# Placing streamed matmul operands at 0xc0 and held ones at 0 modulo 0x100 in a one-core decoder block

## The chip, the cores and the metric

The kernel runs on one core of one Trainium2 chip. The metric is device time in microseconds (us). Engines are named as the profile names them: PE is TensorE's matmul, PEld its weight load (LDWEIGHTS), DVE is VectorE, ACT ScalarE, POOL GpSimd, and SP issues the DMAs. A matmul has two operands in SBUF. One is loaded into the array beforehand by a weight load and is called *held* here; the other is then passed through column by column and is called *streamed*.

## What is computed

One layer of a decoder block on 256 tokens of width 1024, all in float32. The reference, cut to its skeleton:

```python
h = rmsnorm(x, g_pre_mix); z = h @ w_in                 # 1024 x 8248
# NSA: compressed, selected and windowed attention, 16 heads in 4 groups
y_nsa = gb0 * o_cmp + gb1 * o_slc + gb2 * o_win
# mLSTM over chunks with causal conv, gates and head norm
y_ml = sigmoid(o_ml) * h_ml
# cross-attention to 256 memory tokens
y_mem = memory_xattn(q_mem, mem, g_mem, w_mem_kv)
y = gm0 * (y_nsa @ w_proj_nsa) + gm1 * (y_ml @ w_proj_ml) + gm2 * (y_mem @ w_proj_mem)
x = x + rmsnorm(y @ w_out, g_post_mix)
gu = rmsnorm(x, g_pre_ffn) @ w_ffn_in                   # 1024 x 5632
x = x + rmsnorm((silu(gate) * up) @ w_ffn_down, g_post_ffn)
```

## The kernel before

**Numbers in two parts.** Nearly every large product is made in fp32r with both operands split: `split` (two instructions, ACT then DVE) writes `hi`, a rounded copy, and `lo`, the remainder. A product is then hi·hi + hi·lo + lo·hi, three matmuls. Weights come from HBM as 161 units of 128x1024 floats (512 KB each): `fetch` brings a unit to a tile `raw` (4 buffers), `parts` (L659) splits it into `whi` and `wlo` (4 buffers each).

**Four forms of product.** They differ in which operand is held.

- `fmaj` (L674): the weights are held, the activations streamed, 256 columns at a time; 24 matmuls a unit. Used with X = (`hh`, `hl`) for the projections that must come out feature by feature: 28 units and one of gate weights (`gw`). The first product with the memory tokens (`mem_k`) has the same shapes, with `mh` and `ml` streamed.
- `tmaj` (L701): the activations are held, the weights streamed, 512 columns at a time; 12 matmuls a unit. Used for `mem_v`, the values, gates, merge gates, the three branch projections, `w_out`, the first four blocks of the FFN (`ffn_gate`, `ffn_up`) and `ffn_down`.
- `fcat` (L682): for the other 36 units of the FFN input. The activations `xc` hold hi and lo side by side, so weights `hi` are held against 512 streamed columns and `lo` against 256: seven `hi` blocks, eight `lo` blocks, then the last `hi` block.
- Attention: `nsa_half` (L1185) and `ml_head` (L1097) with streamed `kk`, `pTh`/`pTl`, `ce0`/`ce1` and `vml`, of 128 to 272 columns.

**Who sets the order.** All operations are recorded first. The class `Plan` then searches an order of all engines with its own table of durations (`cost`, L238): `schedule` places, `replay` times the result, and `choose` (L532) first tries two values of a per-matmul cost and two of a slack, then makes `ROUNDS` random trials that pull forward work on which PE waited. `issue` (L586) gives out the operations in that order. The order of program work is therefore a result of the cost table and of the number of trials, and so is the buffer of a tag that a tile gets.

**Where tiles lie.** `issue` makes a tile when its first operation is given out, and the pools place slots in that order, `one`, `big`, `wpool`, `work`. In the program before, the start addresses modulo 0x100 are:

| remainder | tiles |
|---|---|
| 0xc0 | `KK` (`memt`, `kk`, `xc`), two of the three `G` (`mh`, `ml`, `qkm1`, `vml`, `u0`, `u2`), `cs` |
| 0 | `hh`, `hl`, `yh`, `yl`, `E` (`ymemt`, `ymlt`, one `wq`), `Y` (`kmem`, `vmem`, `ynh`, `ynl`, `u3`, `u4`, two `wq`), `V` (`vs`, `u5`, one `wq`), `C`, `qs`, the third `G` (`u1`, `qkm0`), all of `raw`, `whi`, `wlo`, `pTl`, `ce0`, `ce1` |
| 0x40 | `vcs` |
| 0xe0 | `pTh` |
| 0x80, 0xa0 | `pp`, `sq` and other work tiles |

Blocks within these tiles begin at multiples of 0x200 or 0x400 bytes, so a block has its tile's remainder; the groups of `kk` are 0x840 apart, and each adds 0x40.

Of the kernel before, what the change touches and what calls it, by code (L numbers as in the profile page):

```python
# [19 lines left out]
P = 128  # L20
# [148 lines left out]
class Plan:  # L169
# [67 lines left out]
    @staticmethod  # L237
    def cost(op):  # L238

        n = op.outs[0].n if op.outs else 0  # L240
        views = op.outs + op.ins
        sources = [v for v in op.ins if not v.tile.psum and v.n > 1]
        wide = op.method in ("tensor_copy", "tensor_scalar") and not any(v.tile.psum for v in op.outs)
        op.port = op.eng == "POOL" and bool(op.ins) or op.eng == "DVE" and len(sources) > 1 - wide
        op.load = 0.0
        if op.dma:
            n = views[0].n * 4
            return views[0].shape[0] * n / (230.0 if n < 2048 else 400.0)
        if op.eng == "PE":
            dtype = op.a[1].dtype  # L250
            op.load = 56.0 if dtype == BF16 else 109.0
            if op.method == "transpose":
                return n / 1.2 + 2
            if dtype == F32:
                return max(1.72 * op.a[1].n, n / 0.6 + 10)
            return n / 2.4 + (2.5 if dtype == BF16 else 13.3) + (100 if op.a[1].shape[0] <= 32 else 0)
        n = max(v.n for v in views)
        psum = any(v.tile.psum for v in views)
        pointers = sum(v.n == 1 for v in op.ins)
        part = any(v.place() != (0, P) and v.shape[0] >= 32 for v in op.outs + [v for v in op.ins if v.n > 1])  # L260
# [12 lines left out]
        return 100 + 1.4 * n if op.method == "tensor_scalar" else max(150.0, 2.1 * n - 70)  # L273
# [80 lines left out]
    def schedule(self, matmul, slack, boost):  # L354
# [50 lines left out]
        while len(order) < len(ops):  # L405
            best = None
            for e, c in avail.items():
                if c:
                    f = max(free[e], dma - self.AHEAD) if e == "SP" else free[e]
                    t = max(f, min(x[0] for x in c))  # L410
                    if best is None or t < best[0]:
                        best = (t, e)
            assert best, "no instruction can be issued"
            now, e = best
            ready = [x for x in avail[e] if x[0] <= now]
            pick = min(ready, key=lambda x: (x[1].urge + (self.SWITCH if x[1].table not in (None, table) else 0)))
            op = pick[1]
            bad = held(op) > now or [t for t in op.tiles if t.real is None and (
                t.tag.next != t.seq or not t.tag.free or t.tag.free[0][0] > now)]
            avail[e].remove(pick)  # L420
            if bad:
                offer(op)
                continue
            op.start = now
            tags = []
            for t in op.tiles:
                if t.real is None:
                    t.place = t.tag.free.pop(0)[1]
                    t.real = True
                    t.tag.next += 1  # L430
                    tags.append(t.tag)
            if op.dma:
                free[e] = now + self.ISSUE
                dma = max(now + self.LAND, dma) + op.cost
                end = dma
            else:
                cost = op.cost
                if e == "PE":
                    now = op.start = max(now, loaded + op.load)
                    loaded = now  # L440
                    if op.load == 109.0 and op.method != "transpose":
                        cost += matmul - 13.3
                end = now + cost
                if op.table not in (None, table):
                    end += self.TABLE
                    table = op.table
                free[e] = end
            op.end = end
            if op.port:
                port[e] = end  # L450
            order.append(op)
            for t in op.tiles:
                if e != "PE":
                    t.busy[e] = op, end
                t.left -= 1
                t.end = max(t.end, end + self.NEXT[op.kind] + slack)
                if not t.left:
                    t.tag.free.append((t.end, t.place))
                    t.tag.free.sort()
                    tags.append(t.tag)  # L460
            for u in op.users:
                strict = u.deps[op]
                u.ready = max(u.ready, end + latency(op, u) if strict else end if op.eng == u.eng else now)
                u.wait -= 1
# [62 lines left out]
            free[e] = op.end  # L527
        return max(op.end for op in order)

    MATMUL, SLACK, PASSES, ROUNDS = (10.0, 13.3), (60.0, 130.0), 3, 40  # L530

    def choose(self):  # L532

# [68 lines left out]
def block_kernel(ctx, tc, order, xN, xT, memN, head, cst, vec, row, wg, w1, w2, W, out):  # L602
# [79 lines left out]
    def fcat(xc, w, ps):  # L682


        hi, lo = unit(w)
        b = lambda k: slice(k * P, (k + 1) * P)
        for k in range(KD - 1):
            PE.matmul(ps, hi[:, b(k)], xc[:, k], start=k == 0, stop=False)
# [9 lines left out]
            fmaj(ps[:, j, :], xs, range(KD), unit((w, 2 * i + j)))  # L698
        return ps

    def tmaj(xs, *key, n=4, ps_new=ps_d, into=None, last=0):  # L701


        ps = [ps_new([P, 512]) for _ in range(2)]
# [9 lines left out]
                PE.matmul(ps[tb], xs[1][:, k, t], hi[:, w], start=False, stop=(k == 2 * n - 1))  # L714

        for u in range(n - last):
            w = unit((*key, u))
            for tb in range(2):
                use(u, tb, w)
        us = range(n - last, n)  # L720
        ws = [unit((*key, u), into and into[u]) for u in us]
        for tb in range(2):
            for u, w in zip(us, ws):
                use(u, tb, w)
# [57 lines left out]

    rw = one.tile([P, 520], F32, name="rw")
    wgt = work.tile([P, 1024], F32, tag="p", bufs=2, name="wgt")
    w2t = one.tile([P, 192], F32, name="w2t")
    part(0, 776)
    part(776, 1544)
    fetch(("mem_k", 1))
# [7 lines left out]
    for u in range(4):  # L796
        if u and ("mem_k", u) not in ready:
            fetch(("mem_k", u))
        raw = ready.pop(("mem_k", u)) if u else mt[:, 264:1288]
        w = [wpool.tile([P, 1024], F32R, tag=t, bufs=4, name=t) for t in ("whi", "wlo")]  # L800
        pieces = HEAD[u]
        for h in range(2):
            if h < pieces:
# [34 lines left out]
        ACT.activation(hh[:, k, :], xt[:, k, :], AF.Copy)  # L838
        DVE.tensor_sub(hl[:, k, :], xt[:, k, :], hh[:, k, :].bitcast(F32))

    vps = tmaj(M, "mem_v", ps_new=ps_s)
    with plan.later(60):
        DVE.tensor_copy(rmb, scale_rows(mn, ps_v([P, S], "rbc"), rm, after=[vps[1].tile.last_pe]))
    with plan.later(150):
# [26 lines left out]
    MC, MT = [msk[:, 384 + 16 * i:400 + 16 * i] for i in range(2)], mtb  # L871


    hid = one.tile([P, 2, NG, 32], F32, name="hid")
    POOL.memset(hid, 0.0)
    for j in range(2):

# [19 lines left out]
        bias = work.tile([P, 1], F32, tag="b1", bufs=2, name="cbias")  # L897
# [6 lines left out]
    gw = [wpool.tile([P, 1024], F32R, tag=t, bufs=4, name="gw") for t in ("whi", "wlo")]  # L904
# [192 lines left out]
    def ml_head(h):  # L1097
# [27 lines left out]
        DVE.tensor_add(num[:, 1, h, :], pn[:, 130:258], num[:, 1, h, :])  # L1125
        DVE.tensor_copy(den[:, :, h:h + 1], pn[:, 0:260].rearrange("p (a d) -> p a d", a=2)[:, :, P:P + 1])
        for tb in range(2):
            junk = work.tile([P, P], F32, tag="junk", bufs=2, name="junk")
            ACT.activation(junk, num[:, tb, h, :], AF.Square, accum_out=ssq[:, tb, h:h + 1])

    ymlt = bigt("E", 2, [P, 2, 4, S], F32R, "ymlt")
    yml = [ymlt[:, i] for i in range(2)]
# [184 lines left out]
    def scaled(name, xs, n, gz, scale, pre, root=False):  # L1317
# [95 lines left out]
    for tb, r in scaled("ffn_down", (Hidden(0), Hidden(1)), KF // 2, ((go, [z2[:, 0, :], z2[:, 1, :]]),), halves(rfd), halves(rf), True):  # L1415
# [118 lines left out]
```

## Time and profile before

| | |
|---|---|
| times of the runs shown | 543.06, 543.06 and 543.47 us; median 543.06 |
| span of the profiled execution, first to last instruction | 540.7 us |
| what lies around it (median less span) | 2.4 us |
| PE instructions | 3116 matmuls, 3116 weight loads |
| DMA, mean over the span | 97.85 MB, 181 GB/s |

The profile gives each instruction's start and duration. Matmuls overlap one another in it: the next starts while the last is still on its way through the array. So what a matmul costs PE in a dense run is not its duration but the distance from its start to the next start, called *spacing* below. All instructions carry one source line (L598, where the order is given out), and groups are told apart by tiles: `pd<-hh,wlo` writes `pd` with `hh` streamed and `wlo` held or the other way round; the columns (256 or 512) tell which. `pd` and `pss` are two kinds of PSUM buffer for the same use.

### The profile page before, as it was taken

The page shows a single profiled execution, that of the slowest core. Times are in us where ns is not written, and L with a number is a line of the kernel's source. Part 1 is how long each engine was busy: PE and PEld are TensorE (multiplying, and loading weights), DVE is VectorE, ACT ScalarE, POOL GpSimd, SP SyncE. Part 2 cuts the span into 40 slices and gives each one's busy share as a digit, 9 for nine tenths or more (in the row PEclk, how much of TensorE's full clock was granted, in tenths as well). Part 3 has the DMA queues.
Part 4 walks back from the last instruction along what each step waited for, and adds up shares of the span by engine and source line. Part 5 has one row for each costly group of instructions (what it writes and reads, how often), then busy time and mean ns, then how long its engine had stood idle before and what let it go on. Part 6 is the DMA issues. An engine that isn't in the chain of part 4 may idle for free.

```text
span 540.7 us, 8802 instructions
## 1 busy us (share of the span) xinstructions
PE 530.9 (98%) x3116; PEld 464.9 (86%) x3116; DVE 414.2 (77%) x900; ACT 340.8 (63%) x682; POOL 30.2 (6%) x43
## 2 busy tenths in 40 slices
PE   9999999999999999999999999999999999999995
PEld 9899998998989889888888888788888888888884
DVE  6795696799999998997987796965777777754543
ACT  7695695566688885966895435744555556653431
POOL 0110000010010111101120000000000000000000
PEclk9999999999999999999999999999999999999999
DMA  8995346525433264254455474834455555555512
GB/s 317 416 412 188 129 136 195 183 79 199 146 137 128 88 234 155 98 177 155 149 174 187 167 257 159 272 118 156 166 190 189 193 196 195 189 187 191 190 63 78
DMA packets 28699, 97.85 MB, mean 181 GB/s; under 512 B 3312, under 2 KB 5232, under 8 KB 28400
## 3 DMA queue, kind: packets, MB, share of 16 engines
q1 hardware_dynamic: 28656, 97.30, 50.6%
q8 instruction: 24, 0.39, 0.3%
q14 instruction: 19, 0.16, 0.1%
HBM read 95.19 MB, written 1.05 MB: 178 GB/s over the span
## 4 chain that ended last, share of the span: by engine, by line
PE 79%; DVE 9%; ACT 5%; DMA 4%; issue 2%; POOL 1%; SPq 0%; DVEq 0%; ACTq 0%
PE pd L598 41%; PE pss L598 27%; DMA raw<-in_W 4%; DVE wlo L598 2%; PE pvn L598 2%; PE sc L598 2%; ACT whi L598 1%; PE ptn L598 1%; PE ph L598 1%; DVE cy L598 1%; ACT L598 1%; DVE sc L598 1%; DVE xt L598 1%; PE psm L598 1%; PE pgf L598 1%
## 5 line engine op out<-in xcount | busy, mean ns | idle before, releaser
L598 DVE TENSOR_TENSOR wlo<-raw,whi 128x1024 fp32r<-128x1024 f32 (+1 forms) x159 | 191.7, 1210 | 83.8 <-ACT whi L598 82.4
L598 ACT ACTIVATE whi<-raw 128x1024 fp32r<-128x1024 f32 (+1 forms) x159 | 166.2, 1051 | 128.8 <-PE pd L598 64.7
L598 PE MATMUL pd<-hh,whi 128*128 128x256 f32 x208 | 59.4, 286 | 0.9 <-DVE on L598 0.9
L598 PE MATMUL pd<-hh,wlo 128*128 128x256 f32 x208 | 59.5, 286 | 0.0
L598 PE MATMUL pd<-hl,whi 128*128 128x256 f32 x208 | 59.2, 285 | 0.0
L598 PE MATMUL pd<-whi,hh 128*128 128x512 f32 x144 | 57.7, 400 | 0.0
L598 PE MATMUL pd<-wlo,hh 128*128 128x512 f32 x144 | 57.5, 399 | 0.0
L598 PE MATMUL pd<-whi,hl 128*128 128x512 f32 x144 | 57.0, 398 | 0.0
L598 PE MATMUL pss<-xc,whi 128*128 128x512 f32 x168 | 43.6, 395 | 0.0
L598 PE MATMUL pss<-whi,u 128*128 128x512 f32 x132 | 42.0, 390 | 0.0
L598 PEld LDWEIGHTS pd<-hh,whi 128*128 128x128 f32 x208 | 39.7, 191 | 1.3 <-DVE on L598 1.1
L598 PEld LDWEIGHTS pd<-hh,wlo 128*128 128x128 f32 x208 | 39.8, 191 | 0.0
L598 PEld LDWEIGHTS pd<-hl,whi 128*128 128x128 f32 x208 | 39.7, 191 | 0.1
L598 PEld LDWEIGHTS pss<-xc,whi 128*128 128x128 f32 x168 | 30.5, 188 | 5.6
L598 PE MATMUL pd<-xc,whi 128*128 128x512 f32 x120 | 32.2, 397 | 0.0
L598 PEld LDWEIGHTS pd<-whi,hl 128*128 128x128 f32 x144 | 27.1, 188 | 4.4
L598 PEld LDWEIGHTS pd<-whi,hh 128*128 128x128 f32 x144 | 27.1, 188 | 4.4 <-ACT cx L598 0.3
L598 PEld LDWEIGHTS pd<-wlo,hh 128*128 128x128 f32 x144 | 27.1, 188 | 4.3 <-DVE wlo L598 0.3
L598 DVE CUSTOM_DVE_ANT_0 sc<-sc,msk 128x16 f32<-128x16 f32 (+2 forms) x96 | 27.2, 316 | 4.2 <-PE sc L598 3.4
L598 PEld LDWEIGHTS pss<-whi,u 128*128 128x128 f32 x132 | 24.8, 188 | 5.3
L598 ACT ACTIVATE pp<-sc,mx 128x128 f32<-128x128 f32 (+1 forms) x64 | 26.7, 427 | 1.5 <-DVE mx L598 1.3
L598 PE MATMUL pss<-wlo,u 128*128 128x512 f32 x66 | 25.8, 390 | 0.0
(333 smaller groups left out, 1122.0 us busy)
## 6 DMA issues: line engine op xcount, KB each, us to landing
raw<-in_W SPq DMA_DIRECT2D x161, 512.0 KB, 3.4
w<-in_w SPq DMA_DIRECT2D x2, 1024.0 KB, 8.1
xn<-in_xN SPq DMA_DIRECT2D x2, 512.0 KB, 9.8
xt<-in_xT SPq DMA_DIRECT2D x2, 512.0 KB, 8.2
mn<-in_memN SPq DMA_DIRECT2D x2, 512.0 KB, 8.8
kk<-kk SPq DMA_DIRECT2D x8, 128.0 KB, 3.1
x<-in_xN SPq DMA_DIRECT2D x2, 512.0 KB, 3.8
memt<-in_head SPq DMA_DIRECT2D x1, 512.0 KB, 6.4
```

Of the source, the lines that this page charges most:

```text
L598: op.ins_ = getattr(op.real, op.method)(*map(arg, op.a), **{k: arg(x) for k, x in op.kw.items()})
```

## The change

Every SBUF tag is given a fixed place ahead of the first operation (`lay_out`). The table `RESIDUE` fixes a remainder for those that feed matmuls; the others follow by size. The buffers of `whi` and `wlo` grow from 1024 to 1088 floats, and a unit is written into them at a shift of 0, 32 or 48 floats (0, 0x80, 0xc0 bytes): 0 where `fmaj` holds it, (32, 0) in `fcat`, 48 by default in `tmaj`, 0 in `mem_v`, and in `ffn_down` 48 only against the `Y` tiles. To make room, `w2t` and `hid` share the slots of `ce0` and `ce1`, `cbias` has one buffer, and the tile `junk` goes (the unused squares are written over the float32 copy of a mask in `msk`, of which a bf16 copy is in use). The planner's durations for fp32r matmuls change from n/2.4 + 13.3 to 17n/38.4 + 1.5 ns, the tried offsets from (10.0, 13.3) to (-3.0, 0.0) on that base, and its random trials from 40 to 100.

```diff
-            return n / 2.4 + (2.5 if dtype == BF16 else 13.3) + (100 if op.a[1].shape[0] <= 32 else 0)
+            return (n / 2.4 + 2.5 if dtype == BF16 else n * 17 / 38.4 + 1.5) + (100 if op.a[1].shape[0] <= 32 else 0)
...
-                        cost += matmul - 13.3
+                        cost += matmul
...
-    MATMUL, SLACK, PASSES, ROUNDS = (10.0, 13.3), (60.0, 130.0), 3, 40
+    MATMUL, SLACK, PASSES, ROUNDS = (-3.0, 0.0), (60.0, 130.0), 3, 100
...
+    FIRST_BYTE = 0x4080
+    RESIDUE = {"vcs": 0, "V": 0, "C": 0, "G": 0, "qs": 0, "KK": 0xC0, "E": 0xC0, "Y": 0xC0, "hh": 0xC0, "hl": 0xC0,
+               "whi": 0, "wlo": 0, "raw": 0, "pT0": 0xC0, "pT1": 0xC0, "ce0": 0xC0, "ce1": 0xC0}
+
+    def lay_out(self, order):
...
+        for name in ("one", "big", "wpool", "work"):
+            pool, slots = pools[name]
+            for (label, n), size in sorted(slots.items(), key=lambda x: (rank.get(x[0][0], 99), x[1])):
+                pad = (self.RESIDUE[label] - place) % 0x100 if label in rank else 0
+                if pad:
+                    pool.tiles.tile([P, pad // 4], F32, tag=f"pad{place}", bufs=1, name="pad")
+                pool.tiles.tile([P, (size + 31) // 32 * 8], F32, tag=f"{label}_{n}", bufs=1, name="slot")
...
+    def room(shift=(0, 0)):
+        return [wpool.tile([P, 1088], F32R, tag=t, bufs=4, name=t)[:, n:n + 1024] for t, n in zip(("whi", "wlo"), shift)]
...
-        hi, lo = unit(w)
+        hi, lo = unit(w, shift=(32, 0))
...
-    def tmaj(xs, *key, n=4, ps_new=ps_d, into=None, last=0):
+    def tmaj(xs, *key, n=4, ps_new=ps_d, into=None, last=0, shift=lambda u: 48):
...
-    w2t = one.tile([P, 192], F32, name="w2t")
+    w2t = work.tile([P, 192], F32, tag="ce0", bufs=1, name="w2t")
...
-    vps = tmaj(M, "mem_v", ps_new=ps_s)
+    vps = tmaj(M, "mem_v", ps_new=ps_s, shift=lambda u: 0)
...
-    hid = one.tile([P, 2, NG, 32], F32, name="hid")
+    hid = work.tile([P, 2, NG, 32], F32, tag="ce1", bufs=1, name="hid")
...
-            junk = work.tile([P, P], F32, tag="junk", bufs=2, name="junk")
-            ACT.activation(junk, num[:, tb, h, :], AF.Square, accum_out=ssq[:, tb, h:h + 1])
+            ACT.activation(msk[:, K_MT - K_M0:], num[:, tb, h, :], AF.Square, accum_out=ssq[:, tb, h:h + 1])
...
+                        shift=lambda u: 48 * (tags[u // 2][0] == "Y")):
```

More of the change, by code (lines that the diff above doesn't have):

```diff
@@ L584, in choose @@
         return self.schedule(matmul, slack, boost)
+    FIRST_BYTE = 0x4080
+    RESIDUE = {"vcs": 0, "V": 0, "C": 0, "G": 0, "qs": 0, "KK": 0xC0, "E": 0xC0, "Y": 0xC0, "hh": 0xC0, "hl": 0xC0,
+               "whi": 0, "wlo": 0, "raw": 0, "pT0": 0xC0, "pT1": 0xC0, "ce0": 0xC0, "ce1": 0xC0}
+    def lay_out(self, order):
+        pools, at = {}, {}
+        for op in order:
+            for t in op.tiles:
+                if not t.psum:
+                    slots = pools.setdefault(t.pool.name, (t.pool, {}))[1]
+                    key = t.label, t.place
+                    n = t.n * (2 if t.dtype == BF16 else 4)
+                    slots[key] = max(slots.get(key, 0), n)
+        place = self.FIRST_BYTE
+        rank = {label: i for i, label in enumerate(self.RESIDUE)}
+        for name in ("one", "big", "wpool", "work"):
[5 more added lines that the diff above has]
+                pool.tiles.tile([P, (size + 31) // 32 * 8], F32, tag=f"{label}_{n}", bufs=1, name="slot")
+                at[label, n] = place + pad
+                place += pad + (size + 31) // 32 * 32
+        self.at, self.end = at, place
     def issue(self):
@@ L592, in issue @@
         with self.tc.manual_schedule():
+            self.lay_out(order)
             for op in order:
@@ L657, in fetch, with parts, unit @@
         return raw
-    def parts(raw, into=None):
-        hi, lo = into or [wpool.tile([P, 1024], F32R, tag=t, bufs=4, name=t) for t in ("whi", "wlo")]
+    def room(shift=(0, 0)):
+        return [wpool.tile([P, 1088], F32R, tag=t, bufs=4, name=t)[:, n:n + 1024] for t, n in zip(("whi", "wlo"), shift)]
+    def parts(raw, into=None, shift=(0, 0)):
+        hi, lo = into or room(shift)
         split(hi, lo, raw)
         return hi, lo
-    def unit(key, into=None):
+    def unit(key, into=None, shift=(0, 0)):
         if key not in ready:
             fetch(key)
-        return parts(ready.pop(key), into)
+        return parts(ready.pop(key), into, shift)
     def mm3(out, ah, al, bh, bl, start, stop, **kw):
@@ L716, in tmaj @@
         for u in range(n - last):
-            w = unit((*key, u))
+            w = unit((*key, u), shift=(shift(u),) * 2)
             for tb in range(2):
@@ L720, in tmaj @@
         us = range(n - last, n)
-        ws = [unit((*key, u), into and into[u]) for u in us]
+        ws = [unit((*key, u), into and into[u], (shift(u),) * 2) for u in us]
         for tb in range(2):
@@ L799, in block_kernel @@
         raw = ready.pop(("mem_k", u)) if u else mt[:, 264:1288]
-        w = [wpool.tile([P, 1024], F32R, tag=t, bufs=4, name=t) for t in ("whi", "wlo")]
+        w = room()
         pieces = HEAD[u]
@@ L896, in block_kernel @@
             PE.matmul(ph, w1t[j][:, l, :], st[:, 2 * l % 16, n:n + 80], start=(l == 0), stop=(l == 15))
-        bias = work.tile([P, 1], F32, tag="b1", bufs=2, name="cbias")
+        bias = work.tile([P, 1], F32, tag="b1", bufs=1, name="cbias")
         DVE.tensor_copy(bias, ph[:, 64:65])
@@ L903, in block_kernel @@
     pgf = ps_s([P, S], "pgf")
-    gw = [wpool.tile([P, 1024], F32R, tag=t, bufs=4, name="gw") for t in ("whi", "wlo")]
+    gw = room()
     split(gw[0], gw[1], wgt)
@@ L1315, in block_kernel, with scaled @@
     DVE.tensor_mul(gp[:, 1, :], g1, gp[:, 0, :])
[L1317 removed]
+    def scaled(name, xs, n, gz, scale, pre, root=False, **kw):
         ss = work.tile([P, 2, 2], F32, tag="ss", bufs=2, name="ss")
@@ L1323, in scaled @@
             c = slice(512 * h, 512 * h + 512)
-            for tb, ps in enumerate(tmaj(xs, name, h, n=n, ps_new=ps_ds, last=4 * h)):
+            for tb, ps in enumerate(tmaj(xs, name, h, n=n, ps_new=ps_ds, last=4 * h, **kw)):
                 sq = work.tile([P, 512], F32, tag="sq", bufs=3, name="sq")
@@ L1414, in block_kernel @@
     halves = lambda t: [t[:, tb:tb + 1] for tb in range(2)]
-    for tb, r in scaled("ffn_down", (Hidden(0), Hidden(1)), KF // 2, ((go, [z2[:, 0, :], z2[:, 1, :]]),), halves(rfd), halves(rf), True):
+    for tb, r in scaled("ffn_down", (Hidden(0), Hidden(1)), KF // 2, ((go, [z2[:, 0, :], z2[:, 1, :]]),), halves(rfd), halves(rf), True,
+                        shift=lambda u: 48 * (tags[u // 2][0] == "Y")):
         for c in (slice(0, 512), slice(512, 768), slice(768, 1024)):
```

## The prediction

> **What bounds the kernel now.** I read the page's busy table and its 40 slices first, then the chain that ended last.
>
> ```profile
> span 540.7 us, 8802 instructions
> ...
> PE 530.9 (98%) x3116; PEld 464.9 (86%) x3116; DVE 414.2 (77%) x900; ACT 340.8 (63%) x682; POOL 30.2 (6%) x43
> ...
> PE   9999999999999999999999999999999999999995
> ...
> PEclk9999999999999999999999999999999999999999
> ...
> PE 79%; DVE 9%; ACT 5%; DMA 4%; issue 2%; POOL 1%; SPq 0%; DVEq 0%; ACTq 0%
> ```
>
> PE is busy in every slice but the last, at full granted clock, and carries 79% of the chain. It idles for 540.7 - 530.9 = 9.8 us, of which 6.6 us is the tail behind the last matmul (533.73 + 0.39, below) and about 1 us the start. So time is won only where the spacing of matmuls shrinks. I therefore went to the timeline of PE alone and looked for dense runs of one form, first and last start with the count between them.
>
> ```profile
> 98.74 0.28 PE L598 MATMUL pd<-hh,wlo 128*128 128x256 f32 x1
> ...
> 102.94 0.28 PE L598 MATMUL pd<-hl,whi 128*128 128x256 f32 x1
> ```
>
> Between these lie 35 matmuls of `fmaj`: (102.94 - 98.74)/35 = 120.0 ns each. Streamed `hh`/`hl` and held `whi`/`wlo` all have remainder 0.
>
> ```profile
> 400.62 1.07 PE L598 MATMUL pd<-xc,wlo 128*128 128x256 f32 x8
> 401.53 2.02 PE L598 MATMUL pd<-xc,whi 128*128 128x512 f32 x8
> 403.39 1.07 PE L598 MATMUL pd<-xc,wlo 128*128 128x256 f32 x8
> 404.30 0.39 PE L598 MATMUL pd<-xc,whi 128*128 128x512 f32 x1
> 404.53 1.80 PE L598 MATMUL pss<-xc,whi 128*128 128x512 f32 x7
> ```
>
> Here `fcat` streams the same 256 columns, from remainder 0xc0 with `wlo` held at 0: eight take (401.53 - 400.62) = 0.91 us, 113.5 ns each. Equal shape and data type, same engine state, 6.5 ns less; the cleanest starts give 113.3, which I use (difference 6.7 ns). Each kind is the same in all its dense runs, whichever buffer it has, so the remainder is the suspect. A second pair of rows, means of single durations by group, says the same: spacing in a dense run is the duration less about 163 ns.
>
> ```profile
> L598 PE MATMUL pd<-hh,wlo 128*128 128x256 f32 x208 | 59.5, 286 | 0.0
> ...
> L598 PE MATMUL pss<-xc,whi 128*128 128x512 f32 x168 | 43.6, 395 | 0.0
> ...
> L598 PE MATMUL pd<-xc,whi 128*128 128x512 f32 x120 | 32.2, 397 | 0.0
> ...
> L598 PE MATMUL pss<-xc,wlo 128*128 128x256 f32 x168 | 22.6, 277 | 0.0
> ...
> L598 PE MATMUL pd<-whi,ynh 128*128 128x512 f32 x24 | 9.3, 389 | 0.0
> ...
> L598 PE MATMUL pss<-wlo,mh 128*128 128x512 f32 x16 | 6.3, 392 | 0.0
> ```
>
> For 512 columns the good pair is another one. `whi` streamed at 0 with `ynh` held at 0 is best (389), `xc` streamed at 0xc0 with `whi` held at 0 worst (395 and 397), `wlo` streamed at 0 with `mh` held at 0xc0 between (392). The two runs that size them:
>
> ```profile
> 318.50 0.39 PE L598 MATMUL pss<-whi,ynh 128*128 128x512 f32 x1
> ...
> 324.40 0.39 PE L598 MATMUL pss<-whi,ynl 128*128 128x512 f32 x1
> ```
>
> ```profile
> 364.22 0.39 PE L598 MATMUL pd<-whi,xc 128*128 128x512 f32 x1
> ...
> 369.94 0.39 PE L598 MATMUL pss<-whi,xc 128*128 128x512 f32 x1
> ```
>
> 26 matmuls in 5.90 us are 226.9 ns (0 streamed, 0 held); 25 in 5.72 us are 228.8 ns (0 streamed, 0xc0 held). For a whole `fcat` unit, 8 wide and 8 narrow matmuls, the rows above give 403.39 - 400.62 = 2.77 us, where 8 x 226.7 + 8 x 113.3 would be 2.72.
>
> My reading: the streamed reads and the next matmul's weight load meet in the memory, and the difference of the two start addresses modulo 0x100 sets how often. That only the difference counts is assumed, not shown: no row has both at 0xc0.
>
> **The change part by part.**
>
> *1. `fmaj`, 29 units x 24 = 696 matmuls.* `hh`/`hl` go to 0xc0, weights stay at 0: the pair of the 113.3 ns row. In full that is 696 x 6.7 = 4.6 us. Thirteen of the units stand beside the attention:
>
> ```profile
> 28.00:104.00 76.00, 75.84 (x589) 73.01 (x588) 56.07 (x107) 53.62 (x97) 2.40 (x6) 1.00 0.59 207
> 104.00:282.00 178.00, 176.81 (x1109) 155.94 (x1108) 161.45 (x510) 135.48 (x352) 22.48 (x20) 1.00 0.42 147
> ```
>
> (Stretch, length, then PE, PEld, DVE, ACT, POOL busy, clock, DMA share, GB/s.) From 28 to 104 us DVE is busy 56.07 of 76 us, so the 16 units there keep the full gain, 384 x 6.7 = 2.6 us. From 104 to 282 us DVE is busy 91% and runs of one form are short; I count 5 ns, 312 x 5 = 1.5 us. If DVE's cover were gone altogether, these 1.5 us would become PE waits for `wlo`. **Taken: -4.1; bounds -4.6 and -2.6.**
>
> *2. `fcat`, 36 units.* `xc` stays at 0xc0, `whi` moves to 0x80, `wlo` stays. The streamed address is then 0x40 ahead of the held one. The nearest row with that difference is 228.8 ns (0 less 0xc0 is 0x40). Seven wide matmuls of a unit take now (403.39 - 401.53) less the one that ends the unit before, 0.226: 1.63 us, 233 ns each. Six of them are followed by a `whi` load and gain 4 ns; the seventh is followed by `wlo` as before, and the two around the last `hi` block get a new neighbour, which I let cost 3 ns each. That is about 20 ns a unit, 36 x 0.020 = 0.7. Clean spacing would give 36 x 0.05 = 1.9; 8 ns on all eight (the 397 row, against 0.05 us a unit now) would cost 0.5. **Taken: -0.8; bounds -1.9 and +0.5.**
>
> *3. Wide matmuls now with 0 streamed, 0xc0 held:* `mem_v` 48, `ffn_gate` 72 of 96, `ffn_up` 48, and `u0`, `u2` of `ffn_down` 96, together 264. They go to equal remainders, 228.8 to 226.9 ns. **Taken: -0.5; bounds -0.6 and 0.** The 24 `ffn_gate` matmuls on `V` stay as they are.
>
> *4. Narrow attention matmuls.* `pTh`, `pTl` and `ce` to 0xc0 against `vs` and `vcs` at 0, and `kmem` against `qm`:
>
> ```profile
> L598 PE MATMUL pvn<-pTh,vs 128*128 128x256 f32 x48 | 13.0, 283 | 0.0
> ...
> L598 PE MATMUL psm<-kmem,qm 128*128 128x256 f32 x24 | 3.5, 283 | 0.0
> ```
>
> 283 against 277 is 6 ns; 152 matmuls, not in long runs: at most 0.9, **taken -0.4**, at least 0. `kk`, 96 matmuls, keeps its remainders and its `qs` at 0.
>
> *5. `mem_k` turns the other way.* `mh`, `ml` go from 0xc0 to 0, so 96 matmuls get the 120 ns pair: +0.6 in full. They lie in the first 12 us, where the start waits for data as well (the chain's first long piece, then the timeline):
>
> ```profile
> 2.12 5.65 DMA raw<-in_W
> ```
>
> ```profile
> 9.06 0.62 PE L598 MATMUL pd<-ml,whi 128*128 128x256 f32 x4
> 9.52 0.62 PE L598 MATMUL pd<-mh,wlo 128*128 128x256 f32 x4
> ```
>
> Four take 0.46 us at 9 us, so PE is dense there by then; the chain has the DMA ahead of it. **Taken +0.3; bounds 0 and +0.6.**
>
> *6. All other wide matmuls* (weights streamed at shift 48 against `hh`, `hl`, `yh`, `yl`, `E`, `Y`, or `xc`): some 890 that have 0/0 now or join that class get 0xc0/0xc0. Same difference, **taken 0**. This is the largest unknown: see the third rival.
>
> *7. Splits.* ACT and DVE write `whi`/`wlo` at 0, 0x80 or 0xc0. Rows of equal shape at other remainders bear on that:
>
> ```profile
> L598 DVE TENSOR_TENSOR pTl<-ptn,pTh 128x512 fp32r<-128x512 f32 x24 | 16.0, 686 | 0.1
> ...
> L598 DVE TENSOR_TENSOR mrg<-mrg 128x512 f32<-128x512 f32 x8 | 5.5, 690 | 0.1
> ```
>
> 686 ns with an input at 0xe0 and the output at 0, 690 with all at 0x80: no effect on DVE. The shared slots of `w2t`, `hid` add waits between work 40 us apart. The squares into `msk` are ACT's own sequence; if they made DVE's mask readers wait, eight squares of some 0.3 us could cost DVE up to 2 us in its fullest stage. Taken 0.
>
> *8. The order.* New durations and 100 trials give another order. What it can win is what PE loses to waits now: 9.8 us idle less 6.6 of tail less 1 of start, 2.2 us, since the tail is fixed work:
>
> ```profile
> 533.73 0.39 PE L598 MATMUL pd<-whi,u 128*128 128x512 f32 x1
> ```
>
> It can lose as much. **Taken 0; bounds -2 and +3.**
>
> Sum: -4.1 - 0.8 - 0.5 - 0.4 + 0.3 = **-5.5 us**. The profiled span of 540.7 becomes 535.2, and with the 2.4 us around it the time is 537.6, against the median of 543.06.
>
> **A rule that speaks against it.** The Trainium skill, "TensorE: Matmul & The Clock Gate", section "Step-by-step: what each phase is for", says that PE has two independent SBUF read ports and that loading the next tile's weights "doesn't steal SBUF read bandwidth from the running matmul". By it the addresses would not matter, and terms 1 to 5 would be nothing. The 120.0 and 113.5 ns above disagree with that, unless something else tells these two forms apart.
>
> **The rivals.**
>
> - *Nothing happens* (chance 5%). The two narrow forms differ also in their rows: `fmaj` changes its streamed block every matmul between `hh` and `hl`, `fcat` walks through one tile. If that makes the 6.7 ns, all terms are 0 and the time is 543.1. Against it: `psm<-kmem,qm`, another kernel stage at 0/0, has 283 too. The rule named above gives this time.
> - *More than forecast* (17%). `fcat` becomes clean (-1.9), terms 1, 3, 4 come in full (-6.1), `mem_k` is hidden, and the longer search wins 0.5: 543.06 - 8.5 = 534.5. For it: the differences are the same in every dense run.
> - *Slower* (7%). One mechanism: what counts is not the difference but the streamed address, and 512 columns streamed from 0xc0 are the bad case, as in `fcat`. Then the 890 wide matmuls of part 6 go from 226.7 to the longer of the two `fcat` rows, 397 against 389, 8 ns more: +7.1 us, 543.06 - 5.5 + 7.1 = 544.7. It decides from 5.5 us / 890 = 6.2 ns each, that is from 232.9 ns on. For it: the only wide matmuls that stream from 0xc0 today have the longest durations, 395 and 397. Against it: narrow ones from 0xc0 have the shortest.
> - *The order eats half* (15%). The search works on other durations, DVE is full at 104 to 282 us, and PE's waits there more than double: +3, 540.6.
>
> **How the numbers follow.** Forecast, 536 to 540: 56%; more than forecast 17%; order eats half 15%; slower 7%; nothing 5%. A measurement of this kernel can tell about 0.2% (1.1 us) from no change. Faster than 541.97 are the forecast, the better case and nearly all of the fourth: 0.86. Nothing, and edges of its neighbours: 0.07. Slower: 0.07. The range from 534.2 to 541.5 leaves out the slower case, no change and the far edge of the better one.
>
> **What would show it.** Step 1: `pd<-hh,wlo` at 277 to 280 ns and dense runs at 113.3. Step 2: the wide `pss<-xc,whi` below 395, three units in less than 8.32 us. Step 3: `wlo,mh` from 392 to 389. Step 5: `mh,whi` runs longer by 6 ns. Step 6: `whi,ynh` still at 389; 395 or more there would be the slower rival and would make the forecast wrong. Step 8: PE's idle time near 9.8 us; DVE waits in the middle stage would show the fourth rival.

## The result and the profile after

The changed kernel takes 537.0 us (median of 4 runs, 536.13 to 537.46) against 543.06 us: a ratio of 0.9886, with an interval from 0.9869 to 0.9902. The forecast was 537.6. The profiled execution took 536.95 us, its span 535.2 us. In a second set of runs, made with the experiments, the same kernel took 536.38 us, a ratio of 0.9892 [0.9878, 0.9906]. The helper that gives out the work is at L627 now.

The page of the changed kernel: busy time, the DMA engines' share in 40 slices, and the chain:

```profile
span 535.2 us, 8817 instructions
...
PE 525.0 (98%) x3116; PEld 462.3 (86%) x3116; DVE 411.9 (77%) x900; ACT 342.2 (64%) x682; POOL 30.8 (6%) x43
...
DMA  8995356525524454344465575734555555555512
...
PE 87%; DVE 5%; DMA 4%; ACT 1%; issue 1%; POOL 0%; SPq 0%; DVEq 0%; ACTq 0%
```

The span falls by 5.5 us, PE's busy time by 5.9. PE now carries 87% of the chain, where it had 79%. Its idle time has not fallen: 535.2 - 525.0 = 10.2 us, 9.8 before. Everything was won inside PE's busy time. The groups of PE of the changed kernel by form (busy us, mean ns of one, idle before):

```profile
L627 PE MATMUL pd<-hh,wlo 128*128 128x256 f32 x208 | 58.5, 281 | 0.0
...
L627 PE MATMUL pss<-xc,whi 128*128 128x512 f32 x168 | 43.1, 392 | 0.0
L627 PE MATMUL pd<-xc,whi 128*128 128x512 f32 x120 | 31.9, 394 | 0.0
L627 PE MATMUL pss<-xc,wlo 128*128 128x256 f32 x168 | 22.6, 277 | 0.0
...
L627 PE MATMUL pvn<-pTh,vs 128*128 128x256 f32 x48 | 13.1, 281 | 0.0
...
L627 PE MATMUL pd<-whi,ynh 128*128 128x512 f32 x24 | 9.3, 389 | 0.0
...
L627 PE MATMUL pss<-wlo,mh 128*128 128x512 f32 x16 | 6.2, 390 | 0.0
...
L627 PE MATMUL psm<-kmem,qm 128*128 128x256 f32 x24 | 3.4, 276 | 0.0
```

`xc,whi` loses 3 ns, `wlo,mh` 2 ns, `psm` 7 ns, and `whi,ynh`, now 0xc0 against 0xc0, stays at 389. `hh,wlo` is the surprise: 281, not the 277 of `xc,wlo`, though both now stream from 0xc0 against 0. Two dense runs of `fmaj` in the timeline of PE, first and last matmul of each, show why. The first:

```profile
99.96 0.28 PE L627 MATMUL pd<-hh,whi 128*128 128x256 f32 x1
...
104.79 0.28 PE L627 MATMUL pd<-hh,wlo 128*128 128x256 f32 x1
```

These are 41 steps in 4.83 us, **117.8 ns** each. The second:

```profile
53.99 0.28 PE L627 MATMUL pd<-hl,whi 128*128 128x256 f32 x1
...
59.78 0.28 PE L627 MATMUL pd<-hl,whi 128*128 128x256 f32 x1
```

These are 51 steps in 5.79 us, 113.5 ns (113.3 after the first few). The same instructions at the same remainders run at one of two speeds, and each of the 20 dense runs of nine steps or more in the trace keeps its speed to its end. The speed isn't set by the program alone: the run of 58 steps that ends at 40.7 us goes at 117.8 ns here, and at 113.3 in a second trace of the same kernel, taken with the experiments. For `fcat`, the starts of its blocks in the same view:

```profile
401.25 1.07 PE L627 MATMUL pss<-xc,wlo 128*128 128x256 f32 x8
402.16 2.00 PE L627 MATMUL pss<-xc,whi 128*128 128x512 f32 x8
404.00 1.07 PE L627 MATMUL pss<-xc,wlo 128*128 128x256 f32 x8
...
406.74 1.07 PE L627 MATMUL pss<-xc,wlo 128*128 128x256 f32 x8
```

Two units take 406.74 - 401.25 = 5.49 us, 2.745 each, where one took 2.77.

**Where the time went.** I took the distance from each fp32r matmul of 256, 272 or 512 columns to the next start, less the best distance seen for its width (113.3, 120.4, 226.7 ns), in both traces. What is over by less than 14 ns I sum as *spacing*, what is over by more as *waits* (a wait for data, a change of form, or, in the first microseconds, matmuls of `mem_k` that still start 213 ns apart):

| us | before | after | difference |
|---|---|---|---|
| spacing, `fmaj` | 4.17 | 1.70 | -2.47 |
| spacing, `fcat`, 512 and 256 columns | 1.90 | 1.06 | -0.84 |
| spacing, wide on `xc`, `u0`, `u2`, `mh`, `ml` | 0.57 | 0.26 | -0.31 |
| spacing, narrow attention (`pvn`, `psm`) | 0.71 | 0.43 | -0.28 |
| spacing, `mem_k` | 0.10 | 0.59 | +0.49 |
| spacing, all | 9.60 | 6.19 | -3.41 |
| waits, all | 13.94 | 11.85 | -2.09 |

Together that is 5.5 us, the fall of the span. The places explain 3.4 us of it. The other 2.1 us are waits, which points to the order; the experiments below test that. They lie around `pvn` (1.64 to 0.63), `yh` (0.74 to 0.19) and `ymlt` (0.66 to 0.19). The second trace of the same kernel has 11.28 us of waits and 5.95 us of spacing. The page counts most of the waits as busy time, since an earlier matmul is still on its way while the next start is late: of the 13.94 us before, only 2.2 us are idle time.

The stretch of the attention, in the view by windows (PE, PEld, DVE, ACT, POOL busy), shows what became of the fear for it:

```profile
104.00:282.00 178.00, 177.77 (x1122) 158.25 (x1121) 161.05 (x512) 138.42 (x355) 23.06 (x20) 1.00 0.45 152
```

DVE is as full as before, and PE's idle time there went from 1.2 to 0.2 us. The idle time that came instead is at the start, in the list of what PE waited for (us in total, times, longest):

```profile
PE rbc L627 <- POOL rm L627: 1.3, 1, 1.3
PE warm L627 <- POOL mhalf L627: 1.0, 1, 1.0
PE pd L627 <- ACT whi L627: 0.8, 1, 0.8
```

In before's list `rbc` stands with 0.2 us and the third isn't listed. Both lie in the first 34 us, in the first three slices, where the DMA engines are busy for 8, 9 and 9 tenths.

### The profile page after: what moved, and what is told of

Its sections match the earlier page's. It is cut to its first block, busy times and chain, and to the rows that moved or that the text cites. A ratio compares the mean times of both kernels' runs of the same rounds, so it can differ in the third digit from the quotient of the medians.

```text
span 535.2 us, 8817 instructions
## 1 busy us (share of the span) xinstructions
PE 525.0 (98%) x3116; PEld 462.3 (86%) x3116; DVE 411.9 (77%) x900; ACT 342.2 (64%) x682; POOL 30.8 (6%) x43
## 4 chain that ended last, share of the span: by engine, by line
PE 87%; DVE 5%; DMA 4%; ACT 1%; issue 1%; POOL 0%; SPq 0%; DVEq 0%; ACTq 0%
PE pd L627 47%; PE pss L627 28%; DMA raw<-in_W 4%; PE pvn L627 3%; PE sc L627 2%; PE ptn L627 2%; PE ph L627 1%; DVE wlo L627 1%; ACT whi L627 1%; DVE xt L627 1%; PE pn L627 1%; PE pvm L627 1%; PE pgf L627 1%; PE psm L627 1%; PE pq L627 1%
## 5 line engine op out<-in xcount | busy, mean ns | idle before, releaser
L627 DVE TENSOR_TENSOR wlo<-raw,whi 128x1024 fp32r<-128x1024 f32 (+1 forms) x159 | 191.8, 1213 | 80.4 <-ACT whi L627 79.9
L627 ACT ACTIVATE whi<-raw 128x1024 fp32r<-128x1024 f32 (+1 forms) x159 | 166.2, 1052 | 116.4 <-PE pd L627 57.2
L627 PE MATMUL pd<-hh,wlo 128*128 128x256 f32 x208 | 58.5, 281 | 0.0
L627 PE MATMUL pd<-hh,whi 128*128 128x256 f32 x208 | 58.4, 281 | 0.0
L627 PE MATMUL pd<-hl,whi 128*128 128x256 f32 x208 | 58.2, 280 | 0.0
L627 PE MATMUL pd<-whi,hh 128*128 128x512 f32 x144 | 57.5, 399 | 0.0
L627 PE MATMUL pd<-wlo,hh 128*128 128x512 f32 x144 | 57.5, 399 | 0.0
L627 PE MATMUL pd<-whi,hl 128*128 128x512 f32 x144 | 56.8, 398 | 0.0
L627 PE MATMUL pss<-xc,whi 128*128 128x512 f32 x168 | 43.1, 392 | 0.0
L627 PE MATMUL pss<-whi,u 128*128 128x512 f32 x132 | 42.0, 390 | 0.0
L627 PEld LDWEIGHTS pd<-hl,whi 128*128 128x128 f32 x208 | 39.3, 189 | 0.2
L627 PEld LDWEIGHTS pd<-hh,whi 128*128 128x128 f32 x208 | 39.2, 188 | 0.2
L627 PEld LDWEIGHTS pd<-hh,wlo 128*128 128x128 f32 x208 | 39.1, 188 | 0.1
L627 PEld LDWEIGHTS pss<-xc,whi 128*128 128x128 f32 x168 | 30.5, 188 | 5.2
L627 PE MATMUL pd<-xc,whi 128*128 128x512 f32 x120 | 31.9, 394 | 0.0
L627 DVE CUSTOM_DVE_ANT_0 sc<-sc,msk 128x16 f32<-128x16 f32 (+2 forms) x96 | 27.2, 313 | 5.2 <-PE sc L627 4.5
L627 PEld LDWEIGHTS pd<-whi,hh 128*128 128x128 f32 x144 | 27.1, 188 | 4.5 <-ACT cx L627 0.2
L627 PEld LDWEIGHTS pd<-whi,hl 128*128 128x128 f32 x144 | 27.1, 188 | 4.5
L627 PEld LDWEIGHTS pd<-wlo,hh 128*128 128x128 f32 x144 | 27.1, 188 | 4.0
L627 PEld LDWEIGHTS pss<-whi,u 128*128 128x128 f32 x132 | 24.8, 188 | 5.2
L627 ACT ACTIVATE pp<-sc,mx 128x128 f32<-128x128 f32 (+1 forms) x64 | 26.9, 434 | 1.8 <-DVE mx L627 1.7
L627 PE MATMUL pss<-wlo,u 128*128 128x512 f32 x66 | 25.7, 389 | 0.0
```

The source lines that it names most:

```text
L627: op.ins_ = getattr(op.real, op.method)(*map(arg, op.a), **{k: arg(x) for k, x in op.kw.items()})
```

## The experiments

Theory A: the difference of the two start addresses, modulo 0x100, sets the spacing, and the order gives about 2 us more. Theory B: the streamed address alone counts. Theory C: the order did it all. Diffs are against the changed kernel. Differences between kernels are taken from their ratios to the kernel before, times 542.5 us, against the changed kernel's 0.9892; each has an uncertainty of about 1 us. Of the variants of the kernel, all but the last two have the changed kernel's order on PE.

**Spacing by itself.** Only series of 24 matmuls from one tile; the streamed block starts at `m`, the held ones at `h`. Each series comes after 9 wide matmuls, directly or with a small one (the entry) between.

```diff
+            tests.append((n, 0, 0x20 * s, e))
...
+    for n, m, h in ((256, 0xC0, 0), (256, 0xC0, 0xC0), (256, 0x80, 0x80), (512, 0xC0, 0), (512, 0xC0, 0xC0),
+                    (512, 0xC0, 0x80), (512, 0x40, 0), (256, 0x40, 0x80)):
+        for e in range(4):
+            tests.append((n, m, h, e))
```

> This kernel leaves out the whole block and writes its input back: it only runs series of 24 fp32r matmuls, of 256 or 512 streamed columns in the order of fmaj (streams alternate hi, lo, hi; the third weight block is another), for eight held remainders 0, 0x20 ... 0xe0 against a streamed remainder 0 and for some pairs with both moved, each after four different entries. Theory (difference of the two start addresses modulo 0x100 counts, two steady states of one pair are possible): difference 0: 120 ns at 256 columns and 226.7 at 512; difference 0xc0: 113.3 or 117.8 at 256 depending on the entry, 233 at 512; difference 0x40: 229 at 512; pairs with the same difference and other addresses have the same spacing. Rival (the streamed address alone counts): pairs with 0xc0/0xc0 behave as 0xc0/0 and not as 0/0. Rival (independent read ports): all 113.3 and 226.7.

Some of the series in its timeline of PE. First 0 against 0x40 (a difference of 0xc0) without and with an entry of 272 columns, then 0xc0 against 0xc0; then the same for 512 columns: 0xc0 against 0, and 0xc0 against 0xc0:

```profile
122.33 2.99 PE L53 MATMUL ta<-t 128*128 128x256 f32 x24
...
127.23 0.28 PE L58 MATMUL entry<-t 128*128 128x272 f32 x1
127.35 2.91 PE L53 MATMUL tb<-t 128*128 128x256 f32 x24
...
451.52 3.03 PE L53 MATMUL te<-t 128*128 128x256 f32 x24
...
492.43 5.76 PE L53 MATMUL te<-t 128*128 128x512 f32 x24
...
523.75 5.61 PE L53 MATMUL ta<-t 128*128 128x512 f32 x24
```

The mean of the last 12 distances of a series in ns, by streamed less held start modulo 0x100, with the spread over the entries:

```
difference     0      0x20   0x40   0x60   0x80         0xa0         0xc0            0xe0
256 columns  120.0  116.7  117.8  120.0  118.2-120.0  117.3-118.5  113.3 or 117.8  118.3-118.8
512 columns  226.7  233.3  228.9  233.3  232.6-233.3  233.8-234.6  233.3           233.3
```

Pairs with equal differences but other addresses agree to 0.1 ns (streamed/held): 0/0, 0x80/0x80 and 0xc0/0xc0 at 256 columns (120.0), 0/0 and 0xc0/0xc0 at 512 (226.7), 0/0xc0, 0xc0/0x80 and 0x40/0 at 512 (228.9). That decides for A's first half and against B: 512 columns streamed from 0xc0 are best against 0xc0. For 256 columns at 0xc0 there are two steady spacings. In the three pairs with that difference the entry of 272 columns led to 113.3 each time and the direct start to 117.8 each time; entries of 160 columns or of four small matmuls gave either.

The Trainium skill says in "SBUF — State Buffer", section "Who interferes with whom", that PE has two read ports, one for the matmul's moving operand and one for the weight load, and that they are independent. This grid disagrees, if that is taken to mean that the two can't disturb each other: with nothing else at work, matmuls that differ in their start addresses alone differ by up to 6.7 ns at 256 columns and 7.9 ns at 512. What in the memory or in PE makes the difference, no run shows.

**The order alone.** The changed planner, every operand at its remainder of before, no shifts.

```diff
-    RESIDUE = {"vcs": 0, "V": 0, "C": 0, "G": 0, "qs": 0, "KK": 0xC0, "E": 0xC0, "Y": 0xC0, "hh": 0xC0, "hl": 0xC0,
-               "whi": 0, "wlo": 0, "raw": 0, "pT0": 0xC0, "pT1": 0xC0, "ce0": 0xC0, "ce1": 0xC0}
+    RESIDUE = {"vcs": 0x40, "V": 0, "C": 0, ("G", 0): 0xC0, ("G", 1): 0xC0, ("G", 2): 0, "G": 0, "qs": 0, "KK": 0xC0, "E": 0, "Y": 0, "hh": 0, "hl": 0,
+               "whi": 0, "wlo": 0, "raw": 0, "pT0": 0xE0, "pT1": 0, "ce0": 0, "ce1": 0}
...
-        hi, lo = unit(w, shift=(32, 0))
+        hi, lo = unit(w)
...
-    def tmaj(xs, *key, n=4, ps_new=ps_d, into=None, last=0, shift=lambda u: 48):
+    def tmaj(xs, *key, n=4, ps_new=ps_d, into=None, last=0, shift=lambda u: 0):
...
```

> The order of the changed kernel, instruction by instruction on PE, with the remainders of before (G 0xc0, 0xc0, 0; E, Y, hh, hl, ce at 0; pTh at 0xe0; vcs at 0x40) and no shifts. If the places gave 3.4 us and the order 2.1 us, as the two traces added up, this is at 540.5 us, 3.5 us over the changed kernel. If the places gave all of the forecast's 5.5 us, it is at 543. If the order gave all, it is at 537.

540.32 us, ratio 0.9961 [0.9947, 0.9975]: the order gives 0.0039 x 542.5 = 2.1 us (with it the shared slots and the squares into `msk`, which this kernel keeps), the places the other 3.7. Its groups are back where they were (`wlo,mh` but for one late matmul of 498 ns, which lifts the mean):

```profile
L627 PE MATMUL pd<-hh,wlo 128*128 128x256 f32 x208 | 59.4, 285 | 0.0
...
L627 PE MATMUL pss<-xc,whi 128*128 128x512 f32 x168 | 43.6, 395 | 0.0
...
L627 PE MATMUL pss<-wlo,mh 128*128 128x512 f32 x16 | 6.4, 399 | 0.0
```

Spacing sums to 9.90 us (before 9.60), waits to 11.41 (before 13.94). Theory C falls, and so does the theory that the places did it all.

**`fmaj` back.** `hh` and `hl` at 0, and the weights that `tmaj` streams against them at shift 0.

```diff
-"hh": 0xC0, "hl": 0xC0,
+"hh": 0, "hl": 0,
...
-        for tb, ps in enumerate(tmaj(X, "o_ml", last=2)):
+        for tb, ps in enumerate(tmaj(X, "o_ml", last=2, shift=lambda u: 0)):
...
```

> The changed kernel with hh and hl (and so yh, yl) back at 0, and their tmaj weights streamed at 0, so that only fmaj changes its pair, from 0xc0/0 to 0/0. If fmaj gave what the trace adds up, 2.5 us, the time is 539.5; with the forecast's 4.1 us it would be 541.1. fmaj's dense runs go to 120.0 ns everywhere.

538.82 us, ratio 0.9937 [0.9922, 0.9952]: `fmaj` is worth (0.9937 - 0.9892) x 542.5 = 2.4 us. Its spacing is 4.27 us here, 1.45 and 1.70 in the two traces of the changed kernel.

**`fcat` back.** Both parts at shift 0.

```diff
-        hi, lo = unit(w, shift=(32, 0))
+        hi, lo = unit(w)
```

> The changed kernel with the hi weights of fcat back at 0. The two traces differ by 0.85 us in fcat, so 537.9 is expected; the forecast's 0.8 gives the same, clean spacing would have given 1.9. Three units go back from about 8.24 to 8.32 us.

537.53 us, ratio 0.9910 [0.9895, 0.9925]: 1.0 us for `fcat`. In the trace its spacing is 1.90 us against 1.06.

**`mem_k` back.** `mh` and `ml` at 0xc0, the wide matmuls against `G` shifted with them.

```diff
-"G": 0,
+"G": 0xC0,
...
-    vps = tmaj(M, "mem_v", ps_new=ps_s, shift=lambda u: 0)
+    vps = tmaj(M, "mem_v", ps_new=ps_s)
...
-                        shift=lambda u: 48 * (tags[u // 2][0] == "Y")):
+                        shift=lambda u: 48 * (tags[u // 2][0] != "V")):
```

> The changed kernel with the three G tiles at 0xc0, mem_v and the G part of ffn_down streamed at shift 48 against them. The trace gives mem_k 0.5 us more conflict than before, so if PE is the bound there, the time falls by 0.5 us against the changed kernel; if the start waits for data, it stays the same. The other pairs stay at difference 0.

A miss: 537.72 us, ratio 0.9914 [0.9901, 0.9928], 1.2 us slower than the changed kernel if anything. The timeline of PE shows `mem_k` faster where it is dense, and waiting for `whi` before that:

```profile
8.06 0.63 PE L627 MATMUL pd<-mh,wlo 128*128 128x256 f32 x4
9.14 0.74 PE L627 MATMUL pd<-mh,whi 128*128 128x256 f32 x4 [0.44 <-ACT whi L627]
...
11.08 0.62 PE L627 MATMUL pd<-ml,whi 128*128 128x256 f32 x4
11.54 0.62 PE L627 MATMUL pd<-mh,wlo 128*128 128x256 f32 x4
```

Four matmuls take 11.54 - 11.08 = 0.46 us, 0.48 in the changed kernel. Its spacing falls from 0.61 to 0.09 us against the second trace of the changed kernel, but its waits rise from 0.44 to 1.52: 0.61 is the late start behind the wait for `whi`, and some 0.5 are starts 213 ns apart ahead of 6.4 us. `fmaj` fell into the slower steady state more often (1.90 us against 1.45). The start waits for data here, so no gain shows. The changed kernel's first trace has the same 1.51 us of waits with the slow `mem_k`. Why this kernel came out slower and not equal isn't settled.

**`fcat` with equal remainders.** `whi` at 0xc0, the best difference for 512 columns taken alone.

```diff
-        hi, lo = unit(w, shift=(32, 0))
+        hi, lo = unit(w, shift=(48, 0))
```

> The changed kernel with the hi weights of fcat at 0xc0, so that wide matmuls have difference 0 there. Six dense wide matmuls of a unit go from 228.9 to 226.7 ns, -13 ns; the one narrow stream during which hi is loaded goes from 0x40 to 0, 117.8 to 120, +2. Sum -11 ns a unit, -0.4 us on 36. If the change of form inside a unit breaks the steady state, the difference is 0 within 0.2 us.

Another miss: 537.67 us, ratio 0.9915 [0.9900, 0.9930], 1.2 us slower where a gain was expected. Its units in the timeline:

```profile
401.66 1.11 PE L627 MATMUL pss<-xc,wlo 128*128 128x256 f32 x8
402.60 2.00 PE L627 MATMUL pss<-xc,whi 128*128 128x512 f32 x8
404.44 1.11 PE L627 MATMUL pss<-xc,wlo 128*128 128x256 f32 x8
...
407.22 1.11 PE L627 MATMUL pss<-xc,wlo 128*128 128x256 f32 x8
```

The eight narrow ones take 0.94 us, not 0.91: they have gone to the 117.8 state. The wide ones take 1.84 us in both. A unit is 2.78 us, not 2.745; 36 times 0.035 is 1.3 us (1.1 by the sum over the trace), enough for the whole loss.

**Mixed units by themselves.** A grid over the two differences that a unit mixes, `hi` and `lo`, in steps of 0x20: units of `fmaj` after three entries, and three units of `fcat`.

```diff
+    for a in range(8):
+        for b in range(8):
+            for e in (0, 1, 3):
+                tests.append(("fmaj", 0x20 * a, 0x20 * b, e))
+            tests.append(("fcat", 0x20 * a, 0x20 * b, 0))
```

> This kernel leaves out the whole block and writes its input back: it runs units of fmaj (24 matmuls) and of fcat (3 units of 16) over a grid of two differences in steps of 0x20, that of the two hi blocks and that of the lo block, fmaj after three entries (six wide matmuls; these and one of 272 columns; these and two plain fp32 ones). Theory (difference between a stream and the weights loaded during it counts, and 0xc0 at 256 columns has two steady states, 113.3 and 117.8 ns): 0xc0/0xc0 ends in either of them by the entry; other pairs of differences have one state, and some of these may be below 117.8 for every entry. For fcat 0x40/0xc0 (the changed kernel) 2.75 us a unit, 0xc0/0xc0 (before) 2.77, 0/0xc0 about 2.74. Rival (the entry does not matter, the order of tiles in the real kernel does): all entries alike.

Mean of the last 12 distances of `fmaj` by entry, and the time of a `fcat` unit, from the starts in its trace (ns):

```
differences hi, lo    fmaj, three entries      fcat unit
0xc0, 0xc0            117.8  113.3  117.8      2773
0x40, 0xc0            113.3  113.3  113.3      2747
0xc0, 0x40            113.3  113.2  113.3      2803
0,    0xc0            117.8  117.8  117.8      2780
0,    0               -      120.0  120.1      2794
others                115.5 to 124.4           2757 to 2827
```

(The first series of 0, 0 is left out: it lies at the start of the kernel, and its first 11 distances are 213 ns.) So the changed kernel has the best of the 64 pairs for `fcat`, and equal remainders are worse than before's pair. For `fmaj` two pairs reach 113.3 from every entry, and the kernel's isn't one of them.

**Locking `fmaj`.** `lo` at shift 32, which makes the differences 0xc0 and 0x40.

```diff
-            fmaj(ps[:, j, :], xs, range(KD), unit((w, 2 * i + j)))
+            fmaj(ps[:, j, :], xs, range(KD), unit((w, 2 * i + j), shift=(0, 32)))
...
-    gw = room()
+    gw = room((0, 32))
```

> The changed kernel with the lo weights of fmaj (and of the gate unit) at 0x80, so that its two differences are 0xc0 for hi and 0x40 for lo. The grid shows 113.3 ns there after every entry, where 0xc0/0xc0 stays at 117.8 after some. If the remaining 1.5 us of conflict in fmaj is this second steady state, dense runs are at 113.3 everywhere and the time falls by 1.2 to 1.5 us against the changed kernel, to about 535.0. If the waits for ACT and DVE take the gain, it stays at 536.4.

536.06 us, ratio 0.9884 [0.9868, 0.9900], span 533.7 us. In the trace the mechanism works: a stretch that ran at 117.8 in the changed kernel's trace (34.02 to 36.38 us there, 20 steps in 2.36) now reads

```profile
33.30 0.28 PE L627 MATMUL pss<-hh,whi 128*128 128x256 f32 x1
...
37.95 0.28 PE L627 MATMUL pd<-hh,wlo 128*128 128x256 f32 x1
```

41 steps in 4.65 us, 113.4 ns. The spacing of `fmaj` falls from 1.45 to 0.54 us. In the time it can't be told from the changed kernel (-0.4 us). One cause shows in the trace: `mem_k`'s waits were 1.52 us in this execution, of which 0.6 are starts 213 ns apart, and 0.44 in the second trace of the changed kernel. From the first start of `fmaj` to the end this execution took 504.4 us, the two of the changed kernel 506.2 and 506.6. That is one execution against two; the median is the lowest of all kernels here, no more.

**The wide matmuls at a bad difference.** The default shift of `tmaj` at 32, so that 768 wide matmuls (720 on `hh`, `hl` and the `y` tiles, 48 of `ffn_up`) stream from 0x80 against 0xc0.

```diff
-    def tmaj(xs, *key, n=4, ps_new=ps_d, into=None, last=0, shift=lambda u: 48):
+    def tmaj(xs, *key, n=4, ps_new=ps_d, into=None, last=0, shift=lambda u: 32):
```

> The changed kernel with the weights of tmaj streamed at 0x80 instead of 0xc0 against tiles at 0xc0: some 720 wide matmuls get difference 0xc0. This is the price of the rival that forecast slower. If the difference counts, each dense one goes from 226.7 to 233.3 ns: +4.5 to +4.8 us, 541. If the streamed address alone counts, 0x80 is another case and nothing says which.

538.25 us, ratio 0.9919 [0.9905, 0.9933]: only 1.5 us slower. Where runs are long the price is in full, as the timeline shows:

```profile
318.41 0.39 PE L627 MATMUL pss<-whi,ynh 128*128 128x512 f32 x1
...
320.98 0.39 PE L627 MATMUL pss<-whi,ynl 128*128 128x512 f32 x1
```

That is 11 steps in 2.57 us, 233.6 ns each, where 226.7 stood. But the spacing of these forms rises by 3.0 us in all, not by 768 x 6.6 ns = 5.1: the 432 matmuls on `hh` and `hl`, in short runs beside the attention, were some 3 ns over the best already (1.30 us) and lose only 1.1 us more. And `fmaj` fell into its better state more often (0.81 us against 1.45), and the waits were 10.40 us against 11.28; the edit doesn't aim at either, and whether the other addresses ahead of `fmaj` led to them isn't settled.

**Trials, and the planner of before.** First 40 trials in place of 100; then the durations, offsets and trials of before, with the new places.

```diff
-    MATMUL, SLACK, PASSES, ROUNDS = (-3.0, 0.0), (60.0, 130.0), 3, 100
+    MATMUL, SLACK, PASSES, ROUNDS = (-3.0, 0.0), (60.0, 130.0), 3, 40
```

> The changed kernel with 40 random trials instead of 100, so another order of all engines from the same durations. If the longer search gave the 2.3 us that the order brought, this is at 538 or above; if the durations gave them, at 536.5 to 537.

537.58 us, ratio 0.9913 [0.9899, 0.9928], 1.1 us slower. But its waits at `mem_k` were 2.40 us in the trace, 2.0 more than in the second trace of the changed kernel, and they are no waits for data:

```profile
8.03 1.05 PE L627 MATMUL pd<-mh,whi 128*128 128x256 f32 x4
8.88 1.05 PE L627 MATMUL pd<-ml,whi 128*128 128x256 f32 x4
...
10.44 0.64 PE L627 MATMUL pd<-mh,whi 128*128 128x256 f32 x4
10.91 0.64 PE L627 MATMUL pd<-ml,whi 128*128 128x256 f32 x4
```

Four matmuls take 8.88 - 8.03 = 0.85 us, and 10.91 - 10.44 = 0.47 two blocks later. The slow ones, 213 ns each, make 2.1 of the 2.40 us. They end at 10.2 us in this trace, at 6.7 in the trace of before, at 5.1 in the first trace of the changed kernel, and the second has none, so the moment can differ between executions of one kernel. From the first start of `fmaj` to the end this execution took 505.5 us, less than the changed kernel's 506.2 and 506.6. Only one of the six executions was traced, so the slower median may have other causes too; what the trials alone give isn't settled.

```diff
-            return (n / 2.4 + 2.5 if dtype == BF16 else n * 17 / 38.4 + 1.5) + (100 if op.a[1].shape[0] <= 32 else 0)
+            return n / 2.4 + (2.5 if dtype == BF16 else 13.3) + (100 if op.a[1].shape[0] <= 32 else 0)
...
-                        cost += matmul
+                        cost += matmul - 13.3
...
-    MATMUL, SLACK, PASSES, ROUNDS = (-3.0, 0.0), (60.0, 130.0), 3, 100
+    MATMUL, SLACK, PASSES, ROUNDS = (10.0, 13.3), (60.0, 130.0), 3, 40
```

> The changed places with the durations, offsets and 40 trials of before. If places and order add, this is 2.3 us over the changed kernel, 538.7; if the order only pays together with the places, it is nearer to 536.4 or above 539.

539.15 us, ratio 0.9942 [0.9928, 0.9956]. The places alone give 0.0058 x 542.5 = 3.1 us, and the planner 2.7 us on top of them. Spacing is 5.82 us, waits 13.87 (before 13.94). With the order alone, above, all four corners are there: 2.1 or 2.7 us for the order, 3.1 or 3.7 for the places. They add within the uncertainty of about 1 us.

## Why the prediction was right

The time was forecast to 0.6 us (537.6 for 537.0), the span to the tenth. The rule that the places were chosen by was right, but the closeness of the sum is luck: two terms were off in opposite directions, `fmaj` by 1.6 us too much and the order by 2.1 to 2.7 us too little.

- **Only the difference counts** (assumed for parts 2, 3 and 6): shown, by the grid of pairs and by `whi,ynh` at 389. The change in the spacing of all forms of part 6 is about 0, as taken. That the streamed reads and the weight load "meet in the memory" stays a reading; no run looks inside.
- **Term 1, `fmaj`: mis-sized.** Taken -4.1, bounds -4.6 and -2.6; measured -2.4 by undoing it and -2.5 in the trace, just outside. The step that failed is the reading of one spacing from the `fcat` row. Its narrow matmuls come each time after wide ones, and sit in the faster of two states; `fmaj` starts after all sorts of work and fell into the slower one in many of its runs. So the loss lies in both stretches: 28 to 104 us was taken with 2.6 us and gave 1.5, 104 to 282 us with 1.5 and gave 1.0 (spacing 2.29 to 0.77 and 1.88 to 0.92), and DVE's cover, for which the second was discounted, shows no part in it: `fmaj`'s own waits there went from 1.10 to 0.68 us. Locking the state, above, won 0.9 us of spacing back. Nor were 4.6 us there to be won: `fmaj`'s spacing before sums to 4.17.
- **Term 2, `fcat`: right.** Taken -0.8; -0.84 in the trace, 1.0 us by undoing it. That 228.8 ns at difference 0x40 is the right neighbour was confirmed by 228.9 in the grid. The clean unit of 2.72 us wasn't there to be had by places: the best of 64 pairs is 2.747.
- **Terms 3 and 4: within their bounds.** -0.31 and -0.28, taken -0.5 and -0.4. The count in part 3 was too high: `ffn_gate` has 48 wide matmuls, not 96, so 228 and not 264 could gain, 0.43 us in full. And `ffn_gate` itself gained nothing (0.11 us of spacing before, 0.16 after); why isn't settled.
- **Term 5, `mem_k`: the spacing right, the price on the path 0 by what was seen.** +0.49 us of spacing, but undoing it won nothing: the other end of its bounds.
- **Part 7, the splits: no cost seen.** `wlo<-raw,whi` takes 1226 ns in its main form, 1223 before, and DVE is as full in the attention as before.
- **Term 8, the order: mis-sized.** Taken 0, bounds -2 and +3; measured -2.1 to -2.7 with an uncertainty of about 1 us, at the edge or just outside. The step that failed is "what it can win is what PE loses to waits now", read from the 2.2 us of idle time. Late starts inside PE's busy time are waits as well: all waits together were 13.94 us before, and some 11.7 of them lay inside busy time.

Of the rivals, *nothing happens* is out by the grid and by 539.15 us with the planner of before; the rule of the Trainium skill, "TensorE: Matmul & The Clock Gate", section "Step-by-step: what each phase is for", that stood behind it is not borne out here. *Slower* named a mechanism that the grid refutes (0xc0/0xc0 is 226.7 ns), and its price of 7.1 us was too high as well: a bad difference cost 768 wide matmuls 3.0 us of spacing, since many weren't at their best. *The order eats half* came out with the other sign. *More than forecast* failed at `fcat` and at `fmaj`'s second state.

## What to carry to other kernels

Where PE is the bound and its matmuls change weights each time, look at the distances between starts, not at durations or idle time: a few ns per matmul, and late starts that the page counts as busy, were the whole gain here. Place streamed and held operands by the difference of their start addresses modulo 0x100, and choose it per form by measuring the form itself, as the kernel mixes it (0xc0 for 256 columns here, 0 for 512, 0x40 with 0xc0 for the mix of both). One dense run may not be the steady state of every run: look at several, with other work ahead of them and in more than one execution, before taking one spacing for all.

## What the runs showed of the hardware that was not expected

- **Two steady states.** 256 columns at a difference of 0xc0 run at 113.3 or 117.8 ns, and stay there: 41 steps at 117.8 and 51 at 113.5 with the same remainders. What came just before has a part in it (the entry of 272 columns led to 113.3 in all three pairs), but one run of the same kernel went at 117.8 in one execution and at 113.3 in another. Two mixed pairs of differences, 0xc0 with 0x40 and the reverse, reached 113.3 from all three entries.
- **The best difference turns with the width.** 0 is the best for 512 columns (226.7) and among the worst for 256 (120.0); 0xc0 is the best for 256 and costs 6.6 ns at 512.
- **A mix has its own optimum.** In `fcat`, `whi` at its own best difference made the `wlo` matmuls slower by 4.5 ns each, and the wide ones no faster in sum.
